# Values and compressed keys of 1024 latent rows by seven quarter products of 400 columns, context rows by a walk over the contraction

## The chip, the cores and the metric

The kernel runs on one core of one Trainium2 chip. The metric is the device time of one execution in microseconds (us). All matrix work is done in a split of 32-bit floats: every operand is kept as a rounded high part and a low part that holds the rest, and a product of two operands is three matmuls (high by high, low by high, high by low), which the helper `mm3` issues.

## The reference, cut to what matters

The layer takes 1024 latent rows and 256 context rows of 1024 numbers: a gated feed-forward half step, one normalised input for two attentions, their merge, and a second half step. The change lies in the input projection of the second part:

```python
qa, ka, va, cq, ckv, kr, gates = jnp.split(h @ w_in, IN_SPLITS, axis=-1)
kv = heads(_rmsnorm(ckv, g_kv) @ w_ukv, N_HEADS_MLA)
```

`va` (512 columns, the values of neighbourhood attention, 8 heads of 64), `ckv` (256 columns, the compressed keys of latent attention) and `kr` (32 columns, its rope keys) are needed for all 1280 rows, so 800 columns of `h @ w_in` over a contraction of 1024. `ckv` is then normalised row by row and multiplied by `w_ukv` for heads of keys and values.

## The kernel before, in words

Engines run their own instruction streams. The kernel is written as one plan: `plan.step` appends a step of TensorE work, and `plan.spread(fs, x, y)` puts side work (casts, subtractions, loads) between the steps numbered x and y. All DMAs are issued by one queue, that of SyncE, in the order of the program; an issue whose data isn't there yet holds up all behind it. `store` hands a write to the queue two steps late. Wide tiles of 128x1024 come from two pools ("u" with 24 buffers and "v" with 16), tiles of 128x512 from a third ("t" with 20), and PSUM banks from three tags (s3, m3 and v2).

A weight piece is loaded, ScalarE casts it to its high part, and VectorE subtracts that for the low part (`split`, `high_low`). The rows of `h` stand the other way round in planes of 128x512 (8 blocks of the contraction by two halves of the rows). `h2` is the planes of the latent rows for the quarter products that stand ahead of this place: a11, a12 and a22, and the sums s1 to s4 of the seven-product scheme. The plane a21 (blocks 0 to 3, rows 512 to 1023) is not among the seven. Before, `fill1` (L467) made its high and low part for the work here and wrote them out through `keep21` (`k21`, 8 stores), and `load21` brought them back.

The work that changes is two sets of ten steps, one step per 128 rows (eight latent tiles, then two context tiles, whose columns come from `hc2`, filled from `xcs` by `hc2_step`):

- `lat_tile(s, t)`: 8 blocks of the contraction by 3 matmuls of 288 columns (ckv and kr). The result is copied out, the row's scale is found (`rstd`), and `scale_row` multiplies and stores the tile to `cks`; `latent_steps` loads the ten tiles back.
- `va_tile(s, t)`: 8 blocks by 3 matmuls of 512 columns, then a cast and a subtraction of 128x512 and 8 stores of 32x8x128 to the four key windows `vws` (one for each block of 16 query columns; rows of 512 bytes, 128 KB a store, 8 tiles by 8 stores). A context tile is one store to `vcs`.

Between the stores of the values the queue issues the four `winT` loads of 512 KB. `side_weight` splits them, and `side_k` takes them for the NA keys of the context rows, four steps right behind the last `va_tile`. Then follow `kv_heads` for the chunks 2 (context), 0 and 1 and `q_heads`. `latent_cols` turns the scaled keys by TensorE. `q_stat` is a step of 8 thin matmuls for the norm of the query rows, put behind the second step of the stage. The seven-product scheme itself (`Quarters`) serves other products of the kernel with quarters 512 columns wide: in its first two products it copies four banks to SBUF with ScalarE (`out`), and in the other five it adds the banks onto them with VectorE.

## Time and profile before

| What | Value |
|---|---|
| median of 3 runs | 2558.57 us (2557.13 to 2559.03) |
| the profiled execution's own time | 2559.15 us |
| its span | 2557.4 us, so 1.75 us lie outside it |
| granted TensorE clock | 0.998 |
| TensorE busy | 2529.0 us (99% of the span), 13416 matmuls |
| VectorE busy | 1936.8 us (76%) |
| ScalarE busy | 1262.8 us (49%) |
| first matmul of the first `lat_tile` | 1157.64 us after the span's start |
| first matmul of the first `side_k` | 1249.42 us |

The table is read from the totals and from the order of TensorE's matmuls in time. A busy TensorE means matmuls one behind the other; "x24" in a row of the timeline counts the matmuls that the row holds, and names such as `bm`, `bs` and `bv` are PSUM banks, `xu`, `xv` and `t` tiles of the pools, `d` memory of the chip.

### The profile page before, as it was taken

Reading aid. Unit: us, or ns where it says so; the run is one execution under the profiler, and the core shown is the slowest. Engines: PE = TensorE matmul, PEld = TensorE weight load, DVE = VectorE, ACT = ScalarE, POOL = GpSimd, SP = SyncE. Lnnn points to the kernel's source line nnn. Section 1 sums busy time; section 2 is a strip of 40 time slices with the busy share of each in tenths; the row PEclk is TensorE's granted clock in tenths of the full one; section 3 lists DMA queues with packets and bytes.
Section 4 is the critical chain, followed back from the end, with each engine's and each line's share of the span. In section 5 each row is a group of like instructions: output and inputs, shape, how many; then the busy total and the mean of one; then the engine's idle time right before and its main releaser. Section 6 shows DMA issues by size and latency. Waiting matters only on the chain.

```text
span 2557.4 us, 38229 instructions
## 1 busy us (share of the span) xinstructions
PE 2529.0 (99%) x13416; PEld 2159.6 (84%) x13416; DVE 1936.8 (76%) x3629; ACT 1262.8 (49%) x2375; POOL 218.6 (9%) x372
## 2 busy tenths in 40 slices
PE   8999999999999999999999999999999999999998
PEld 6888888888898888889889999998888888888887
DVE  4789996887786577874568988887886888767777
ACT  5632233445654753433448988783266322233444
POOL 1000000001000000001003522221011000000003
PEclk9999999999999999999999999999999999999999
DMA  8455643943674666755978733206836445326724
GB/s 307 153 177 190 200 146 119 340 146 132 226 272 141 212 232 222 242 183 177 302 282 292 232 91 77 68 7 244 311 131 211 156 157 169 111 99 234 273 70 165
DMA packets 245761, 479.47 MB, mean 187 GB/s; under 512 B 30465, under 2 KB 71617, under 8 KB 245569
## 3 DMA queue, kind: packets, MB, share of 16 engines
q1 hardware_dynamic: 245568, 477.02, 55.5%
q8 instruction: 106, 1.74, 0.3%
q14 instruction: 87, 0.70, 0.1%
HBM read 348.93 MB, written 127.99 MB: 186 GB/s over the span
## 4 chain that ended last, share of the span: by engine, by line
PE 84%; ACT 6%; DVE 6%; issue 3%; DMA 1%; POOL 0%; SPq 0%; POOLq 0%; DVEq 0%; ACTq 0%
PE bs L154 36%; PE bm L154 26%; PE bv L154 19%; PE bm L157 2%; ACT xu L1914 2%; DVE xu L1778 2%; DVE t L1941 1%; ACT t L1940 1%; ACT t L120 1%; PE bs L157 1%; DVE xv L120 1%; DVE xu L120 1%; ACT t L1914 1%; DVE t L120 1%; ACT xu L120 0%
## 5 line engine op out<-in xcount | busy, mean ns | idle before, releaser
L120 ACT CAST xu<-t 128x512 fp32r<-128x512 f32 (+1 forms) x270 | 161.4, 603 | 493.4 <-DVE t L120 351.3
L154 PE MATMUL bm<-xu,xu 128*128 128x512 f32 (+2 forms) x1572 | 366.6, 386 | 0.0
L154 PE MATMUL bs<-xv,xu 128*128 128x512 f32 x1488 | 357.4, 389 | 0.3 <-DVE t L120 0.3
L154 PEld LDWEIGHTS bm<-xu,xu 128*128 128x128 f32 x1572 | 288.0, 188 | 56.7 <-ACT t L120 0.2
L154 PE MATMUL bv<-xv,xu 128*128 128x512 f32 x1342 | 335.5, 389 | 0.0
L154 PEld LDWEIGHTS bs<-xv,xu 128*128 128x128 f32 x1488 | 279.1, 188 | 59.0 <-issue 1.1
L154 PEld LDWEIGHTS bv<-xv,xu 128*128 128x128 f32 x1342 | 251.8, 188 | 52.2
L154 PE MATMUL bs<-xv,xv 128*128 128x512 f32 x1086 | 265.9, 390 | 0.0
L120 DVE TENSOR_TENSOR xu<-xu,xu 128x512 fp32r<-128x512 f32 (+1 forms) x296 | 202.3, 688 | 59.2 <-ACT xu L120 58.7
L154 PEld LDWEIGHTS bs<-xv,xv 128*128 128x128 f32 x1086 | 203.0, 188 | 41.7
L154 PE MATMUL bs<-xu,xu 128*128 128x512 f32 (+1 forms) x972 | 226.2, 381 | 0.0
L120 DVE TENSOR_TENSOR t<-t,t 128x512 f32<-128x512 f32 (+2 forms) x278 | 185.3, 674 | 45.1 <-ACT t L120 36.1
L154 PE MATMUL bs<-w,w 96*128 96x512 f32 (+3 forms) x832 | 206.9, 368 | 3.1 <-DMA w<-d 1.8
L154 PEld LDWEIGHTS bs<-xu,xu 128*128 128x128 f32 x972 | 177.4, 188 | 35.7 <-issue 1.4
L120 POOL TENSOR_SCALAR st<-st 128x1 f32<-128x1 f32 (+1 forms) x66 | 34.7, 526 | 1888.7 <-ACT t L120 1870.4
L120 ACT CAST xv<-t 128x512 fp32r<-128x512 f32 x170 | 106.1, 624 | 167.5 <-PE bv L154 69.0
L120 DVE TENSOR_TENSOR xu<-t,xu 128x512 fp32r<-128x512 f32 (+1 forms) x270 | 179.5, 665 | 10.7 <-ACT xu L120 10.6
L154 PE MATMUL bm<-xv,xv 128*128 128x512 f32 x690 | 182.9, 390 | 0.0
L120 ACT CAST xu<-xu 128x512 fp32r<-128x512 f32 x218 | 133.2, 619 | 74.0 <-DMA xu<-in_wo 46.6
L120 DVE TENSOR_TENSOR xv<-t,xv 128x512 fp32r<-128x512 f32 x170 | 117.2, 690 | 65.0 <-ACT xv L120 64.5
L154 PE MATMUL bv<-t,w 128*128 128x256 f32 x896 | 150.2, 288 | 2.2 <-DVE t L1941 1.6
L154 PEld LDWEIGHTS bm<-xv,xv 128*128 128x128 f32 x690 | 129.2, 188 | 27.1 <-issue 0.4
(246 smaller groups left out, 4238.2 us busy)
## 6 DMA issues: line engine op xcount, KB each, us to landing
d<-t SPq DMA_DIRECT2D x366, 256.0 KB, 2.6
t<-d SPq DMA_DIRECT2D x274, 256.0 KB, 3.9
xu<-in_f1w SPq DMA_DIRECT2D x59, 512.0 KB, 4.2
xu<-in_f2w SPq DMA_DIRECT2D x58, 512.0 KB, 3.8
t<-in_wada SPq DMA_DIRECT2D x112, 256.0 KB, 5.2
xv<-in_f1w SPq DMA_DIRECT2D x44, 512.0 KB, 6.8
xu<-in_winT SPq DMA_DIRECT2D x38, 512.0 KB, 4.9
w<-d SPq DMA_DIRECT2D x32, 512.0 KB, 6.3
```

Source lines behind the costliest of these rows:

```text
L120: return lambda *x, **y: pin(f(*x, **y))
L154: return pin(nc.tensor.matmul(o, s, m, start=start, stop=stop, skip_group_check=open_group[0]))
L157: return pin(nc.tensor.transpose(o, x, i))
L1778: nc.vector.tensor_scalar(dst, src, 1.0, FMIN, op0=ALU.mult, op1=ALU.max, accum_out=m)
L1914: nc.scalar.activation(x, x, AF.Exp, bias=n_[:, s:s + 1], accum_out=l[:, i:i + 1])
L1940: nc.scalar.copy(t[0], pb)
L1941: nc.vector.tensor_tensor(t[1], pb, f32(t[0]), op=ALU.subtract)
```

## The change

`TokenQuarters` takes the 1024 latent rows by the seven-product scheme. The 800 columns are put in two halves of 400: the first is values 0 to 383 and 16 columns of `ckv`, the second the other 240 columns of `ckv`, the 32 of `kr` and values 384 to 511. With the two halves of the contraction and the two halves of the rows that makes four quarters on each side. Each of the seven products has four blocks of the contraction by four row tiles by three matmuls of 400 columns, a step per block, so 28 steps. Left operands are planes of `h2` that exist already. Right operands are the weight quarters b11, b21, b12 and b22 and four sums t1 to t4 (16 subtractions by VectorE). A weight block is loaded by two DMAs, of which eight have rows of 16 columns. The a21 plane is neither kept nor loaded.

A row tile is complete when its last product is: tiles 0 to 3 behind the fifth, 4 to 7 behind the seventh. The fifth, sixth and seventh products gather in the same four banks: the fifth ends with step 19, the sixth with step 23, behind each VectorE adds the banks onto SBUF, and the seventh goes on a row tile at a time (steps 24 to 27), each in one bank. `done(t)` then copies the rope keys, finds the scale, and makes the values' high and low parts in two pieces (6 heads and 2 heads), with the stores of before. The compressed keys stay in SBUF, `cks` is gone.

The context rows are eight steps (`context_step`), one for each block of the contraction: two row tiles by three matmuls of 512 and three of 288 columns, into four banks that stay open for eight steps. Their weights are loaded a second time, in four pairs (`context_load`). `hc2_step` moves to steps 17 to 24 of the token part, the order of the heads becomes 0, 1, 2, and the `winT` loads are put at steps 3 to 6 of the context part, into pool "v".

On SyncE's queue the last loads ahead of `side_k` stand like this before (`d_369` to `d_372` are the four windows, and a name `xu_...` the values of one row tile, two stores to each window):

```order
L132 DMA d_369<-xu_11510 32x8x128 x2
L132 DMA d_370<-xu_11510 32x8x128 x2
L132 DMA d_371<-xu_11510 32x8x128 x2
L132 DMA d_372<-xu_11510 32x8x128 x2
L132 DMA xu_11662<-in_winT 128x1024
L132 DMA d_369<-xu_11567 32x8x128 x2
L132 DMA d_370<-xu_11567 32x8x128 x2
L132 DMA d_371<-xu_11567 32x8x128 x2
L132 DMA d_372<-xu_11567 32x8x128 x2
L132 DMA xu_11709<-in_winT 128x1024
```

and now like this:

```order
L132 DMA d_368<-xu_11610 32x8x128 x2
L132 DMA d_369<-xu_11610 32x8x128 x2
L132 DMA d_370<-xu_11610 32x8x128 x2
L132 DMA d_371<-xu_11610 32x8x128 x2
L132 DMA d_368<-xu_11657 32x8x128 x2
L132 DMA d_369<-xu_11657 32x8x128 x2
L132 DMA d_370<-xu_11657 32x8x128 x2
L132 DMA d_371<-xu_11657 32x8x128 x2
L132 DMA xv_11775<-in_winT 128x1024
L132 DMA xv_11812<-in_winT 128x1024
L132 DMA xv_11833<-in_winT 128x1024
L132 DMA xv_11847<-in_winT 128x1024
```

The four loads stood behind the values of tiles 3, 4, 5 and 6; now all four stand behind the values of the last latent tile. The first stores themselves stand on the same queue between the loads of the context weights, now:

```order
L132 DMA xv_11402<-in_wva 128x1024
L132 DMA xv_11404<-in_wc 128x704
L132 DMA d_368<-xu_11340 32x8x128 x2
L132 DMA d_369<-xu_11340 32x8x128 x2
L132 DMA d_370<-xu_11340 32x8x128 x2
L132 DMA d_371<-xu_11340 32x8x128 x2
L132 DMA d_368<-xu_11375 32x8x128 x2
L132 DMA d_369<-xu_11375 32x8x128 x2
L132 DMA d_370<-xu_11375 32x8x128 x2
L132 DMA d_371<-xu_11375 32x8x128 x2
L132 DMA xv_11497<-in_wva 128x1024
L132 DMA xv_11499<-in_wc 128x704
```

The pair behind the stores of tiles 0 and 1 is blocks 2 and 3 of the context weights; the pair of blocks 4 and 5 comes behind tiles 2 and 3, that of blocks 6 and 7 behind tile 4. Before, these weights were one load for all ten tiles and stood ahead of every store.

On VectorE the values' low parts stood with the splits of later weights before (128x8x64 is a row tile's values, `xu_11470` a high and low part for the heads):

```order
L120 TENSOR_TENSOR xu_11438<-bs_11413,xu_11438 128x8x64
L120 TENSOR_TENSOR xu_11467<-bm_11442,xu_11467 128x8x64
L120 TENSOR_TENSOR xu_11470<-xu_11408,xu_11470 128x512
L120 TENSOR_TENSOR xu_11473<-xu_11408,xu_11473 128x512
L120 TENSOR_TENSOR xu_11510<-bs_11485,xu_11510 128x8x64
```

and now, where the sixth product ends and the seventh begins (`bs_11211` to `bm_11214` are its four banks, `xv_11427` and `xv_11429` the low parts of the last two weight blocks):

```order
L120 TENSOR_TENSOR xu_11375<-xu_11054,xu_11375 128x2x64
L120 TENSOR_TENSOR xv_11380<-xu_10848,xv_11380 128x400
L120 TENSOR_TENSOR t_11252<-t_11398,t_11248 128x256
L120 COPY kr<-xu_11056 128x32
L120 TENSOR_SCALAR xu_11054<-xu_11054,st_11372 128x256
L120 TENSOR_TENSOR xu_11414<-xu_11056,xu_11414 128x6x64
L120 TENSOR_TENSOR xu_11414<-xu_11056,xu_11414 128x2x64
L120 TENSOR_TENSOR xu_10971<-xu_10971,bs_11211 128x400
L120 TENSOR_TENSOR xu_10973<-xu_10973,bs_11212 128x400
L120 TENSOR_TENSOR xu_10975<-xu_10975,bs_11213 128x400
L120 TENSOR_TENSOR xu_10977<-xu_10977,bm_11214 128x400
L120 TENSOR_TENSOR xv_11427<-xu_10873,xv_11427 128x400
```

The adds that free the banks, and the low parts for the last steps, stand behind the values of tile 2, whose casts come from ScalarE.

The diff, cut to its core:

```diff
         ORDER = (("a11", "b11"), ("a12", "b21"), ("s1", "t1"), ("s4", "b22"), ("s2", "t2"), ("s3", "t3"), ("a22", "t4"))
         BANKS = (("s", "s", "s", "m"), ("m", "m", "v", "v"))
-        LAST = 4
+        WIDTH, SECOND, YKEY = 512, 512, "v"
...
-    def lat_tile(s, t):
-        pb = s.product(t)
-        x = T2()
-        vec.tensor_copy(x[:, :288], pb)
-        vec.tensor_copy(kr[:, t, :], x[:, 256:288])
-        scale_row()
-        scaled_rows.append((t, x[:, 0:256], rstd(x[:, 0:256], 256)))
-
-    def va_tile(s, t):
-        pb = s.product(t)
+    def latent_out(t, x, keys):
+        vec.tensor_copy(kr[:, t, :], keys)
+        scale_latent()
+        ck[t] = x
+        scaled.append((x, rstd(x, 256)))
+    def values_out(t, pieces):
         v = U(F32R)
         vv = v.rearrange("p (h c) -> p h c", h=NH)
-        pv = pb.rearrange("p (h c) -> p h c", h=NH)
-        split_to(vv[:, :, 0:64], vv[:, :, 64:128], pv)
+        for h, src in pieces:
+            pv = src.rearrange("p (h c) -> p h c", c=64)
+            hs = slice(h, h + pv.shape[1])
+            split_to(vv[:, hs, 0:64], vv[:, hs, 64:128], pv)
...
+    class TokenQuarters(Quarters):
+        WIDTH, SECOND, YKEY = 400, 400, "u"
...
+        def load_b(self, name, p):
+            t = self.slot(name, p)
+            k = 4 * (int(name[1]) - 1) + p
+            v, c = (k % 2) * 512, (k % 2) * 352
+            if name[2] == "1":
+                ld(t[:, 0:384], a["wva"][k // 2][:, v:v + 384])
+                ld(t[:, 384:400], a["wc"][2][k // 2][:, c + 64:c + 80])
+            else:
+                ld(t[:, 0:272], a["wc"][2][k // 2][:, c + 80:c + 352])
+                ld(t[:, 272:400], a["wva"][k // 2][:, v + 384:v + 512])
+        def cast(self, n):
+            self.raw[n] = cast(self.slot(self.ORDER[n // 4][1], n % 4), self.WIDTH, "t" if n < 16 else "v")
+        def split(self, n):
+            x, src = self.raw.pop(n)
+            low(*x, src)
+            self.sp[n] = self.h.f[self.ORDER[n // 4][0]][n % 4], x
+        def plan(self, plan):
+            o = len(plan.main)
+            for n in range(self.n):
+                x = min(o + n - 3, o + self.tail[n][0] - 1 if n in self.tail else o + n)
+                plan.early(lambda n=n: self.cast(n), x)
+                plan.spread([lambda n=n: self.split(n)], x, x + 1)
+                plan.step(lambda n=n: self.step(n))
+            for p in range(4):
+                for name, x in (("b11", p - 7), ("b21", p - 3), ("b12", p - 3), ("b22", p + 2)):
+                    plan.spread([lambda name=name, p=p: self.load_b(name, p)], o + x, o + x + 1)
+                for name, x in (("t1", 2), ("t2", 9), ("t3", 13), ("t4", 16)):
+                    plan.spread([lambda name=name, p=p: self.sum(name, p)], o + x + p, o + x + p + 1)
+            return o
+        def done(self, t):
+            y = self.ys[t]
+            latent_out(t, y[:, 384:640], y[:, 640:672])
+            values_out(t, ((0, y[:, 0:384]), (6, y[:, 672:800])))
+    cxr, cxw, cxb = {}, {}, {}
+    def context_load(j):
+        cxr[j] = load(a["wva"][j], key="v"), load(a["wc"][2][j], 704, "v")
+    def context_split(k):
+        v, c = cxr[k // 2]
+        o = (k % 2) * 512, (k % 2) * 352 + 64
+        cxw[k] = split(v[:, o[0]:o[0] + 512], 512, "v"), split(c[:, o[1]:o[1] + 288], 288, "v")
+    def context_step(k):
+        if k == 0:
+            for t in range(2):
+                cxb[t] = PB("v"), PB("m")[:, :288]
+        open_group[0] = True
+        for t in range(2):
+            for pb, w in zip(cxb[t], cxw[k]):
+                mm3(pb, hc2[0].get(k, t * P, P), w, k == 0, k == KD - 1)
+        open_group[0] = False
+        del cxw[k]
+        if k == KD - 1:
+            for t in range(2):
+                x = T2()
+                vec.tensor_copy(x[:, :288], cxb[t][1])
+                latent_out(8 + t, x[:, 0:256], x[:, 256:288])
+            for t in range(2):
+                values_out(8 + t, ((0, cxb[t][0]),))
...
-    sets = [(2, Set(a["wc"][2], 352, "u", "v", 64), range(10)), (None, Set(a["wva"], 512, "v", "u"), range(10))]
+    plan.spread([lambda: ld(rope, a["rope"])], len(plan.main) - 2, len(plan.main) - 1)
+    ys3 = {}
+    tokens = TokenQuarters(h2, ys3)
+    lat_at = tokens.plan(plan)
     o = len(plan.main)
-    lat_at = o
-    plan.spread(sets[0][1].loads(), o - 9, o - 3)
-    plan.spread(sets[0][1].steps(), o - 5, o)
-    plan.spread([load_c, load21, lambda: ld(rope, a["rope"])], o - 2, o)
-    ck = {}
-    for x, (c, s, ts) in enumerate(sets):
-        o = len(plan.main)
-        for t in ts:
-            plan.step((lambda s=s, t=t: va_tile(s, t)) if c is None else (lambda s=s, t=t: lat_tile(s, t)))
-        if x == 0:
-            plan.spread([lambda k=k: hc2_step(k) for k in range(KD)], o + 2, o + 7)
-        if x + 1 < len(sets):
-            plan.spread(sets[x + 1][1].loads(), o, o + 1)
-            plan.spread(sets[x + 1][1].steps(), o + 1, len(plan.main))
-    va_at = o
+    c_at = o
+    plan.step(*[lambda k=k: context_step(k) for k in range(KD)])
+    plan.spread([load_c], lat_at + 13, lat_at + 14)
+    def context_banks(x):
+        banks[0] = x
+    plan.spread([lambda: context_banks("mm")], lat_at + 16, lat_at + 17)
+    plan.spread([lambda k=k: hc2_step(k) for k in range(KD)], lat_at + 17, lat_at + 25)
+    plan.spread([lambda: context_banks("ss")], c_at, c_at + 1)
+    plan.spread([lambda: context_banks("ms")], c_at + 8, c_at + 9)
+    for j in range(4):
+        plan.spread([lambda j=j: context_load(j)], c_at - 6 + 2 * j, c_at - 5 + 2 * j)
+        plan.spread([lambda j=j: tokens.done(j)], lat_at + 20 + j, lat_at + 21 + j)
+        plan.spread([lambda j=j: tokens.done(4 + j)], lat_at + 25 + j, lat_at + 26 + j)
+    for k in range(KD):
+        plan.spread([lambda k=k: context_split(k)], c_at - 3 + k, c_at - 2 + k)
...
-    lat = {(ci, "c"): latent_steps(ci, ck, cks, 256) for ci in range(3)}
...
-    o = va_at
-    plan.spread([scale_row], o, o + 1)
-    plan.spread([f for ci in (2, 0, 1) for f in [lat[ci, "c"]]], o + 3, o + 4)
-    plan.spread([lambda k=k: raw_load(("kv", k), a["wukv"][k]) for k in range(2)], o, o + 1)
-    plan.spread([lambda k=k: wukv.append(kv_weight(k)) for k in range(2)], o + 2, o + 4)
-    plan.spread([f for ci in (2, 0, 1) for f in calls(latent_cols(ci, 6, 8, ck, "u", ckv[ci]), 2)], o + 6, o + 10)
-    plan.spread([lambda i=i: raw_load(("k", i), a["winT"][4 + i]) for i in range(4)], o + 6, o + 10)
-    plan.spread([lambda i=i: side_weight(i) for i in range(4)], o + 8, o + 12)
+    o = c_at
+    plan.spread([lambda k=k: raw_load(("kv", k), a["wukv"][k]) for k in range(2)], o - 4, o - 3)
+    plan.spread([lambda k=k: wukv.append(kv_weight(k)) for k in range(2)], o, o + 2)
+    plan.spread([scale_latent], o + 1, o + 2)
+    for ci, x in ((0, 2), (1, 4), (2, 9)):
+        plan.spread(calls(latent_cols(ci, 6, 8, ck, "u", ckv[ci]), 2), o + x, o + x + 2)
+    plan.spread([scale_latent], o + 8, o + 9)
+    plan.spread([lambda i=i: raw_load(("k", i), a["winT"][4 + i], 1024, "v") for i in range(4)], o + 3, o + 7)
+    plan.spread([lambda i=i: side_weight(i) for i in range(4)], o + 6, o + 10)
     plan.step(*[lambda i=i: side_k(side_w[i], i) for i in range(4)])
     o = len(plan.main)
-    plan.step(*calls(kv_heads(2, ckv[2]), 7))
-    plan.spread([lambda d=d: xq.append(load(cqx[d], key="v")) for d in range(6)], o - 4, o - 2)
-    plan.spread([lambda d=d: q_cols(0, d) for d in range(6)], o - 2, o + 7)
+    plan.step(*calls(kv_heads(0, ckv[0]), 9))
+    plan.spread([lambda d=d: xq.append(load(cqx[d], key="v")) for d in range(6)], o - 3, o)
+    plan.spread([lambda d=d: q_cols(0, d) for d in range(6)], o, o + 9)
     o = len(plan.main)
-    plan.step(*calls(kv_heads(0, ckv[0]), 9))
+    plan.step(*calls(kv_heads(1, ckv[1]), 9))
     plan.spread([lambda k=k: raw_load(("q", k), a["wuq"][k], QR) for k in range(6)], o - 6, o + 6)
     plan.spread([lambda k=k: wuq.append(q_weight(k)) for k in range(6)], o - 3, o + 9)
     o = len(plan.main)
-    plan.step(*calls(kv_heads(1, ckv[1]), 9))
-    plan.spread([lambda d=d: q_cols(1, d) for d in range(6)], o + 2, o + 14)
+    plan.step(*calls(kv_heads(2, ckv[2]), 7))
+    plan.spread([lambda d=d: q_cols(1, d) for d in range(6)], o, o + 12)
     plan.spread([lambda: qrow.append(gate_rows(qstat[1]))], len(plan.main) - 2, len(plan.main) - 1)
     plan.step(*calls(q_heads(0, cqn[0]), 9))
```

91 lines of the change are left out of this document (19 added, 72 removed).

## The prediction

> **What bounds the kernel now.** I read the page's totals first, then the chain of work that ended last.
>
> ```profile
> span 2557.4 us, 38229 instructions
> PE 2529.0 (99%) x13416; PEld 2159.6 (84%) x13416; DVE 1936.8 (76%) x3629; ACT 1262.8 (49%) x2375; POOL 218.6 (9%) x372
> PE 84%; ACT 6%; DVE 6%; issue 3%; DMA 1%; POOL 0%; SPq 0%; POOLq 0%; DVEq 0%; ACTq 0%
> ```
>
> TensorE is the bound: 28 us of the span aren't its work. The change touches one stage, from the first `lat_tile` to the first `side_k`. So I read TensorE's timeline there.
>
> ```profile
> 1157.64 3.32 PE L154 MATMUL bm<-xu,xu 128*128 128x288 f32 x24
> 1160.80 3.32 PE L154 MATMUL bs<-xu,xu 128*128 128x288 f32 x24
> 1167.12 0.38 PE L157 MATMUL bs<-ident,xv 128*128 128x128 f32 x2
> 1167.34 0.38 PE L157 MATMUL bm<-ident,xv 128*128 128x128 f32 x2
> 1167.55 1.84 PE L154 MATMUL bv<-strip,t 128*128 128x1 f32 x16
> 1169.26 3.01 PE L154 MATMUL bs<-xu,xu 128*128 128x288 f32 x21
> 1192.77 5.62 PE L154 MATMUL bm<-xv,xu 128*128 128x512 f32 x24
> 1198.22 1.98 PE L154 MATMUL bs<-xv,xu 128*128 128x512 f32 x8
> 1249.42 11.75 PE L154 MATMUL bm<-t,xu 128*128 128x256 f32 x96
> ```
>
> A tile starts 3.16 us behind the one before it, so a matmul of 288 columns takes 131.7 ns; 5.45 us make 227 ns for 512 columns. The turns for `hc2` take 0.22 us a block, `q_stat` 1.7 us. I count from T0 = 1157.64: `side_k` starts at T0+91.8. Next, what the other engines and the DMAs do in this stage (columns: window, its length and TensorE, its weight loads, VectorE, ScalarE, GpSimd, granted clock, DMA share, GB/s):
>
> ```profile
> 1157.60:1192.80 35.20, 35.20 (x274) 35.16 (x274) 18.47 (x47) 16.94 (x44) 8.79 (x21) 1.00 0.43 153
> 1192.80:1249.40 56.60, 56.60 (x261) 46.92 (x261) 15.04 (x30) 11.56 (x23) 0.74 (x2) 1.00 0.84 226
> 1261.00:1290.00 29.00, 29.00 (x149) 24.41 (x148) 24.34 (x44) 22.18 (x46) 0.00 (x0) 1.00 0.98 352
> ```
>
> TensorE is full from end to end and VectorE and ScalarE are half free, but the DMAs are 84% busy in the second half, and 98% in the heads that follow. So the stage has a second bound close below. What fills it are the 64 stores of the values:
>
> ```profile
> 1210.80 12.40 SPq L132 DMA_DIRECT2D d<-xu  x24
> 1211.00:1223.00 12.00, 12.00 (x55) 9.93 (x54) 4.70 (x12) 2.22 (x4) 0.00 (x0) 1.00 0.97 254
> DMA packets 5987, 3.04 MB, mean 254 GB/s; under 512 B 371, under 2 KB 5987, under 8 KB 5987
> ...
> DMA packets 743, 2.06 MB, mean 411 GB/s; under 512 B 82, under 2 KB 82, under 8 KB 743
> 1226.00:1250.00 24.00, 24.00 (x120) 20.02 (x119) 6.84 (x12) 6.24 (x13) 0.00 (x0) 1.00 1.01 290
> ```
>
> The first three are a stretch with these stores alone (three tiles, 24 stores): 0.517 us a store, with the DMA engines 97% busy at 254 GB/s, so the engines are the limit and not the issue. The fourth is a stretch of 4 us from 1159 on with loads in rows of 4 KB: 411 GB/s. The fifth mixes both, and adding up fits it: 6.96 MB, of which four `winT` loads are 2.10 MB and take 5.1 us at 411, the other 4.86 MB take 19.1 us at 254, in sum 24.2 of 24.0 us.
>
> **The change part by part.**
>
> *TensorE's work.* Removed: 240 matmuls of 288 columns (31.6 us) and 240 of 512 (54.5 us), 86.1 us. Added: 7 x 4 x 4 x 3 = 336 matmuls of 400 columns. The trace has none; between 131.7 and 227 ns a straight line gives 131.7 + 112 x 0.425 = 179.3 ns, in sum 60.2 us. Context: 8 x 2 x 3 = 48 of each old kind, 17.2 us. Together 77.4 us, 8.7 us less. It lies wholly on the path, since TensorE never waits here. `q_stat` (1.7 us) and the turns of `hc2` (8 x 0.22 = 1.7) are issued in both; what is left of the 91.8, 2.3 us, are the 20 turns of the scaled keys. Sixteen of them (1.8) stand ahead of `side_k` still, and 0.5 us go behind it.
>
> *VectorE and ScalarE in the quarters.* Added are 28 low parts, 16 sums and 20 adds of 400 columns on VectorE, about 0.56 us each by the rows below and the 288-column low part's smaller size: 36 us; 16 low parts go (about 9 us). With the 33.5 us of the two windows that is some 60 of 77 us. ScalarE goes from 28.5 to about 45 us. Both fit, so I cost their work at nothing as long as its order holds; TensorE is the cover.
>
> ```profile
> 1161.49 0.42 ACT L120 ACTIVATE t<-t 128x256 bf16<-128x256 f32 x1 [1.96 <-DVE t L120]
> 1161.82 0.19 ACT L120 ACTIVATION_READ_ACCUMULATOR t<-t 128x1 f32 x1
> 1168.23 1.00 ACT L120 ACTIVATE t<-bs,mod,a 128x256 f32<-128x256 f32 x2
> 1198.42 0.59 ACT L120 CAST xu<-bm 128x512 fp32r<-128x512 f32 x1 [4.37 <-PE bm L154]
> 1199.05 0.69 DVE L120 TENSOR_TENSOR xu<-bm,xu 128x512 fp32r<-128x512 f32 x1 [5.14 <-ACT xu L120]
> ```
>
> *Bank hand-overs.* Where a product follows another in the same four banks, bank 0 was finished 9 matmuls earlier: 1.6 us, against one copy or add of 0.6. No wait, while VectorE comes at once. At step 24 it doesn't: the add that frees bank 0, and the low parts of the last two blocks, stand behind the values of tile 2, whose casts stand on ScalarE behind the two activations of `hc2`. The price is between 0 and what is queued, 0.69 + 4 x 0.56 + 2 x 0.56 = 4.0 us. I take 1.6, since VectorE works this queue off while the sixth product still runs.
>
> So TensorE would be ready for `side_k` at 60.2 + 17.2 + 1.7 + 1.7 + 1.8 + 1.6 = T0+84.2, 7.6 us earlier, of which 0.5 come back: -7.1.
>
> *The stores of the values.* They were spread over `va_tile`, from 1199.76 on. Now the first is possible when tile 0 is whole, behind step 19, and ScalarE gets to it only behind the activations of `hc2` whose turns stand behind step 20: 21 x 2.15 = 45.2, plus 1.7 and 4 x 0.22 make T0+47.8; then 1.0, 0.42 + 0.19, 0.6 and 0.7 of the rows above, and a wait or two on VectorE: T0+51. From there 64 stores are 33.0 us by the row of 24. Tiles come faster (one per step of 2.15 us) than their 4.1 us of transfer, so the DMA engines stay full.
>
> *The `winT` loads.* All four now stand on SyncE's queue behind the 64 stores, and so do three of the four pairs of context weights (0.52 + 0.36 = 0.885 MB each) and `wukv` (1.05 MB). Ahead of the end of the first `winT` load are 2.65 + 1.05 + 0.52 = 4.2 MB, 10.3 us at 411. So it ends at 51 + 33.0 + 10.3 = T0+94.3; with about 1.2 us until the landing is seen and the cast and low part (0.6 + 0.7, of which the low part is needed later), `side_k` starts at about T0+96. The context steps that wait for their pairs (blocks 4 and 6, some 2 us) lie inside this wait. Transfer times, for scale:
>
> ```profile
> xu<-in_winT SPq DMA_DIRECT2D x4, 512.0 KB, 4.9
> xu<-in_wukv SPq DMA_DIRECT2D x2, 512.0 KB, 3.9
> xu<-in_wc SPq DMA_DIRECT2D x4, 32.0 KB, 2.2
> ```
>
> The last row is the nearest to the eight new loads of 16 columns (8 KB). They are issued four steps and more ahead, 8 us against 2.2: nothing. If they were ten times as slow they would hold the first steps by up to 5 us.
>
> *What goes without a gain.* The 20 transfers of `cks` and the 12 of the kept plane were on no path that TensorE waited for. Those of `cks` were 2.6 MB on the DMAs of this stage; they leave room there, but ahead of T0+51, where there is room already. The heads' order changes nothing in amount. The `wuq` loads, behind the same queue, come 1 to 3 us late to heads whose DMAs were 98% busy: between 0 and 4 us, and I take 1.
>
> *The sum,* against the profiled execution's 2559.15 us (0.6 above the median of the runs): `side_k` from T0+91.8 to T0+96, +4.3; turns behind it +0.5; heads +1. 2559.15 + 5.8 = **2565 us**. The gain of 7.1 us on TensorE is there, and a wait of 11 to 12 us for `winT` is more.
>
> **The rivals.**
>
> *The stores don't limit, the kernel is faster.* If they moved at the 411 GB/s of the loads, 8.39 MB would take 20.4 us and not 33.0, the first `winT` would be in at T0+82 to 83, and TensorE wouldn't wait: 2559.15 - 7.1 = 2552. It decides at about 370 GB/s: from there on more than 5 us of gain are left. Against it is the row of 254 GB/s at a share of 97%, the same pieces in the same direction. For it speaks that nothing says how much of that share is the reads of other work.
>
> The Trainium skill's page "DMA: Bandwidth & Descriptors" (section Specifications) puts the piece from which a transfer runs at line rate at 512 bytes, which is the size of a row of these stores, and the limit of a core at about 358 GB/s. By it the 64 stores would take an estimated 23.4 us, and the kernel would be at 2554 to 2556. The trace disagrees: 254 GB/s for pieces of 512 bytes against 411 for rows of 4 KB, both with full engines.
>
> *Gain and wait cancel.* If the first store goes out 4 to 6 us earlier than I have it (ScalarE takes tile 0 ahead of the `hc2` activations), the wait shrinks to 6 or 7 us: 2558 to 2561. Against it: both stand in ScalarE's own order, activations first.
>
> *The heads pay as well.* The backlog lasts 5 us longer than before when the heads begin, and `xq` and `wuq` (6 loads each) feed splits on a VectorE busy 24.34 of 29 us. If the splits come late by the whole backlog and not by a part of it, the heads add 5 to 8 us: 2569 to 2573.
>
> **How the numbers follow.** 0.2% (5.1 us) is about what a measurement of this kernel can tell from no change: same is 2553.5 to 2563.7. My forecast (2561 to 2569) has 0.47, of which 0.09 lie within the bound; the faster rival 0.19, 0.02 of it within; cancelling 0.18; the heads 0.16. So faster 0.17, same 0.29, slower 0.54. The likeliest case alone is 2561 to 2569; the range takes in most of the others: 2552.5 to 2571.
>
> **What would show it.** Right: a wait of TensorE of some 10 us ahead of the first `side_k`, ended by `winT`'s landing through ScalarE; no idle time of TensorE in the first 24 steps; 400-column matmuls 179 ns apart; the DMAs near full from T0+51 to T0+95 at 250 to 300 GB/s. A wait of 1 to 2 us at step 24 would be the tail. Wrong: stores above 350 GB/s, `side_k` at T0+84, or idle time inside the quarters, for which I have no price.

## The result and the profile after

The changed kernel takes 2570.79 us (median of 6 runs, 2569.12 to 2571.78), the kernel before 2557.70 in runs beside it: a ratio of 1.0053, 95% interval 1.0042 to 1.0063. It is slower by 13 us. The profiled execution took 2570.67 us, its span is 2568.9, against 2557.4 before: 11.5 us. The totals of the profile page:

```profile
span 2568.9 us, 38214 instructions
PE 2524.9 (98%) x13368; PEld 2160.0 (84%) x13368; DVE 1960.9 (76%) x3687; ACT 1275.6 (50%) x2417; POOL 224.0 (9%) x372
```

TensorE has less work by its count of matmuls and idles 44 us instead of 28. Its timeline in the stage (start, duration, what ran, and in brackets the idle time ahead and what ended it):

```profile
1157.19 1.80 PE L154 MATMUL bs<-t,xu 128*128 128x400 f32 x9
...
1159.37 1.78 PE L154 MATMUL bs<-t,xu 128*128 128x400 f32 x9
1160.99 0.70 PE L154 MATMUL bm<-t,xu 128*128 128x400 f32 x3
1161.53 1.78 PE L154 MATMUL bs<-t,xu 128*128 128x400 f32 x9
...
1213.40 1.54 PE L154 MATMUL bs<-xv,xu 128*128 128x400 f32 x7 [0.79 <-DVE xu L120]
1215.33 1.18 PE L154 MATMUL bs<-xv,xu 128*128 128x400 f32 x5 [0.38 <-DVE xv L120]
...
1216.49 4.57 PE L154 MATMUL bs<-xv,xu 128*128 128x400 f32 x24
1220.89 2.32 PE L154 MATMUL bm<-xv,xu 128*128 128x400 f32 x12
1223.06 0.86 PE L154 MATMUL bv<-xv,t 128*128 128x512 f32 x3
...
1235.54 1.95 PE L154 MATMUL bv<-xv,t 128*128 128x512 f32 x3 [2.72 <-ACT xv L120]
...
1257.04 8.57 PE L154 MATMUL bm<-t,xu 128*128 128x256 f32 x48 [8.50 <-ACT xu L120]
1265.45 0.38 PE L157 MATMUL bm<-ident,t 128*128 128x128 f32 x2
...
1271.63 1.55 PE L154 MATMUL bm<-xu,xu 128*128 128x512 f32 x6
...
1300.16 1.64 PE L154 MATMUL bs<-xu,xu 128*128 128x512 f32 x6 [1.14 <-DVE t L120]
...
1303.62 2.42 PE L154 MATMUL bs<-t,xu 128*128 128x256 f32 x18
```

Before, the rows that answer to the last two (the first product of the heads, then of `q_heads`) are these:

```profile
1261.01 0.88 PE L154 MATMUL bm<-xu,xu 128*128 128x256 f32 x6
...
1290.44 2.42 PE L154 MATMUL bs<-t,xu 128*128 128x256 f32 x18
```

The token part is what was forecast: it ends 65.9 us behind its first matmul, with 1.2 us of wait at step 24 and 180 ns for a matmul of 400 columns (the 12 of a step in 2.16 us, from 1159.37 to 1161.53). Then come a wait of 2.7 us in the context steps and one of 8.5 us ahead of `side_k`. The queue of SyncE and the cast that lets `side_k` go, and the windows (columns as in the prediction):

```profile
1208.12 8.42 SPq L132 DMA_DIRECT2D d<-xu  x16
...
1218.61 11.27 SPq L132 DMA_DIRECT2D d<-xu  x16
...
1230.99 5.52 SPq L132 DMA_DIRECT2D d<-xu  x8
...
1251.88 1.80 SPq L132 DMA_DIRECT2D xv<-in_winT  x4
```

```profile
1256.37 1.14 ACT L120 CAST xu<-xv 128x512 fp32r<-128x512 f32 x2 [10.44 <-issue]
```

```profile
1222.00:1232.00 10.00, 10.00 (x58) 8.96 (x57) 7.64 (x21) 4.98 (x14) 6.97 (x4) 1.00 1.04 304
1232.00:1238.00 6.00, 3.28 (x13) 2.41 (x13) 2.42 (x5) 2.88 (x7) 0.00 (x0) 0.77 1.07 306
...
1248.50:1257.10 8.60, 0.10 (x2) 0.06 (x1) 0.08 (x1) 0.73 (x2) 0.00 (x0) 0.72 0.98 277
1252.30:1262.50 10.20, 5.46 (x24) 5.23 (x25) 4.66 (x11) 4.15 (x10) 1.64 (x4) 0.50 0.96 339
1257.10:1266.00 8.90, 8.90 (x53) 8.67 (x54) 6.96 (x15) 5.19 (x14) 1.64 (x4) 0.70 0.97 328
1262.50:1266.00 3.50, 3.50 (x31) 3.50 (x31) 2.38 (x5) 1.76 (x5) 0.00 (x0) 1.00 1.02 258
```

The first store goes out at T0+50.9, the first `winT` at T0+94.7, it is cast at T0+99.2, and `side_k` starts at T0+99.85 (T0 is the stage's first matmul, here 1157.19). The granted clock behind the wait is 0.70 (0.50 up to 1262.5, then 1.00), and 48 matmuls that take 5.8 us at full clock take 8.4.

The runs below are compared by three starts on TensorE, counted from T0 as read from each run's own timeline. They vary far less than the whole time: before, and in the two variants of it that leave the path alone, `q_heads` starts at 132.80 each time, while the rest, from `q_heads` to the end, spreads from 1264.6 to 1270.5 us without a pattern (but for the last two runs).

| | `side_k` | its four steps | heads | `q_heads` | median us (before beside it) |
|---|---|---|---|---|---|
| before | 91.78 | 11.59 | 29.43 | 132.80 | |
| after | 99.85 | 14.59 | 31.99 | 146.43 | 2570.79 (2557.70) |
| winT first | 91.56 | 13.61 | 33.74 | 138.91 | 2563.31 (2556.29) |
| loads first | 88.18 | 13.49 | 37.42 | 139.09 | 2563.48 (2556.29) |
| kept busy | 99.32 | 14.32 | 31.67 | 145.31 | 2571.23 (2556.29) |
| before, winT last | 93.36 | 17.41 | 29.44 | 140.21 | 2565.69 (2556.29) |
| half the stores | 85.03 | 12.62 | 31.46 | 129.11 | 2554.08 (2557.12) |
| before, half the stores | 91.78 | 11.59 | 29.43 | 132.80 | 2556.28 (2557.12) |
| before, weights twice | 91.77 | 11.59 | 32.96 | 136.32 | 2560.41 (2557.12) |
| loads and wuq first | 88.25 | 16.03 | 36.98 | 141.26 | 2563.18 (2557.12) |
| rows of 4 KB | 99.21 | 14.76 | 32.41 | 146.38 | 2568.98 (2557.08) |
| rows of 4 KB, winT first | 91.56 | 13.40 | 33.62 | 138.58 | 2562.16 (2557.08) |
| before, rows of 4 KB | 91.78 | 11.60 | 29.42 | 132.80 | 2557.00 (2557.08) |
| one pair of weights | 94.23 | 14.31 | 32.27 | 140.81 | 2564.33 (2557.08) |
| stores by GpSimd | 96.79 | 21.61 | 31.38 | 149.78 | 2575.19 (2556.82) |
| the same, 4 KB | 93.82 | 19.98 | 31.87 | 145.67 | 2572.24 (2556.82) |
| stores of 64 KB | 95.66 | 14.82 | 32.94 | 143.42 | 2568.06 (2556.82) |
| a quarter, one pair | 85.06 | 12.62 | 32.12 | 129.80 | 2555.16 (2556.82) |
| stored once | 85.05 | 12.63 | 32.36 | 130.04 | 2584.06 (2556.62) |
| stored once, wuq first | 85.05 | 12.63 | 31.70 | 129.38 | 2582.94 (2556.62) |

### The profile page after: what moved, and what is told of

Its sections match the earlier page's. It is cut to its first block, busy times and chain, and to the rows that moved or that the text cites. A ratio compares the mean times of both kernels' runs of the same rounds, so it can differ in the third digit from the quotient of the medians.

```text
span 2568.9 us, 38214 instructions
## 1 busy us (share of the span) xinstructions
PE 2524.9 (98%) x13368; PEld 2160.0 (84%) x13368; DVE 1960.9 (76%) x3687; ACT 1275.6 (50%) x2417; POOL 224.0 (9%) x372
## 4 chain that ended last, share of the span: by engine, by line
PE 38%; ACT 5%; DVE 5%; issue 2%; DMA 1%; SPq 0%; POOL 0%; POOLq 0%; DVEq 0%; ACTq 0%
PE bs L154 17%; PE bm L154 11%; PE bv L154 8%; ACT xu L1926 2%; DVE xu L1790 2%; PE bm L157 2%; DVE t L1953 1%; ACT t L1952 1%; DMA t<-in_wada 1%; ACT t L1926 1%; ACT t L1766 0%; DMA xu<-in_wuq 0%; ACT t L120 0%; PE bs L157 0%; DVE xu L120 0%
## 5 line engine op out<-in xcount | busy, mean ns | idle before, releaser
L154 PE MATMUL bm<-xu,xu 128*128 128x512 f32 (+1 forms) x1500 | 356.6, 391 | 0.0
L154 PE MATMUL bs<-xv,xu 128*128 128x512 f32 (+1 forms) x1452 | 347.6, 388 | 1.5 <-DVE xu L120 0.8
L154 PEld LDWEIGHTS bm<-xu,xu 128*128 128x128 f32 x1500 | 278.2, 188 | 56.8 <-ACT t L120 0.4
L154 PE MATMUL bs<-xv,xv 128*128 128x512 f32 (+1 forms) x1134 | 274.8, 388 | 0.0
L120 DVE TENSOR_TENSOR xu<-xu,xu 128x512 fp32r<-128x512 f32 (+4 forms) x316 | 209.9, 670 | 64.6 <-ACT xu L120 64.3
L120 DVE TENSOR_TENSOR t<-t,t 128x512 f32<-128x512 f32 (+2 forms) x278 | 185.4, 674 | 43.8 <-ACT t L120 34.5
L154 PE MATMUL bs<-xu,xu 128*128 128x512 f32 (+1 forms) x900 | 216.2, 389 | 1.1 <-DVE t L120 1.1
L154 PEld LDWEIGHTS bs<-xu,xu 128*128 128x128 f32 x900 | 167.6, 188 | 37.4 <-DVE t L120 1.6
L154 PE MATMUL bm<-xv,xv 128*128 128x512 f32 (+1 forms) x690 | 182.7, 388 | 0.0
L120 ACT CAST xu<-xu 128x512 fp32r<-128x512 f32 (+1 forms) x226 | 133.8, 602 | 74.6 <-DMA xu<-in_wo 56.9
L154 PE MATMUL bm<-t,xu 128*128 128x256 f32 (+1 forms) x1252 | 157.9, 287 | 8.5 <-ACT xu L120 8.5
L154 PEld LDWEIGHTS bm<-t,xu 128*128 128x128 f32 x1252 | 154.9, 194 | 9.0 <-ACT xu L120 8.7
```

The costliest lines, as they stand in the source:

```text
L120: return lambda *x, **y: pin(f(*x, **y))
L154: return pin(nc.tensor.matmul(o, s, m, start=start, stop=stop, skip_group_check=open_group[0]))
```

## The experiments

**Where the loads stand.** Theory: the wait at `side_k` is the place of the `winT` loads behind the stores, and the slow matmuls come of the wait. Rivals: the DMAs are the bound whatever the order; the order alone does it, backlog or not.

```diff
 # winT first
-    ... raw_load(("k", i), a["winT"][4 + i], 1024, "v") ..., o + 3, o + 7)
+    ... raw_load(("k", i), a["winT"][4 + i], 1024, "u") ..., o - 9, o - 8)
 # loads first: also
-    context_load(j) at c_at - 6 + 2 * j;  wukv at o - 4
+    context_load(j) at c_at - 8 + j (the last pair in "u");  winT at o - 5;  wukv at o - 8
```

> The changed kernel with one part moved: the four winT loads are issued ahead of the first store of the values (in tiles of pool u). Theory (the wait of 8.50 us ahead of the first side_k is the place of these loads behind the 64 stores, and the slow matmuls behind it, 8.57 us for 48 against 5.8 at full clock, come of the wait): the wait and the slow matmuls go, side_k starts at about 1248.5 us instead of 1257.04, 8.5 + 2.7 us less: 2559 to 2561. The wait of 2.7 us in the context steps stays. Rival (the DMA engines are the bound whatever the order, so the wait only moves into the heads): side_k starts earlier but the heads wait more, the kernel gains under 5 us: 2566 or more.

> The changed kernel with all loads that the stage needs ahead of the stores or behind the first tile's: the four pairs of context weights, wukv, and winT behind the stores of tile 0. Theory: TensorE has no wait from step 24 to side_k, and what the first run leaves (2.7 us of wait and some 3 us of slow matmuls in the context steps) goes too: side_k at about 1243, 2553 to 2556, some 3 to 5 us faster than the kernel before the change. Rival (the DMA engines are the bound): the heads, whose loads stand behind all 64 stores, give it back: 2561 or more.

With `winT` first the wait at `side_k` and the low clock there are gone, 8.3 us, as the theory has it; the kernel is still 7 us slower than before (ratio 1.0027, 1.0017 to 1.0037), and the 2559 to 2561 of the theory were missed. With all loads first `side_k` comes another 3.4 us earlier, and `q_heads` not at all: the heads take 37.4 us instead of 33.7. So the rival holds for what is left, as far as these two runs go. ScalarE's waits in the heads, before, then in these two runs:

```profile
ACT xu L120 <- DMA xu<-in_wuq: 1.5, 2, 1.3
```

```profile
ACT xu L120 <- DMA xu<-in_wuq: 6.9, 5, 1.6
```

```profile
ACT xu L120 <- DMA xu<-in_wuq: 8.0, 5, 1.8
```

The `wuq` loads stand behind the stores too. I read these rows so that the casts that wait for them hold up the casts that free the heads' banks; a run that issues `wuq` earlier tries it below.

**The clock.** 63 matmuls of 256 columns fill the wait:

```diff
         pb = PB("m")
+        for x in range(21 if i == 0 else 0):
+            y = hc2[0].get(x % 8)
+            mm3(pb[:, :NCTX], [z[:, 0:P] for z in y], y, True, True)
```

> The changed kernel with 63 matmuls of 256 columns more, ahead of the first side_k, whose results the first matmul of side_k overwrites: TensorE works for some 7.6 us of the 8.5 us of the wait. Theory (the granted clock falls while TensorE waits, and side_k pays for it): the 48 matmuls of side_k take 5.8 to 6.2 us instead of 8.57, and the kernel is 2.4 to 2.8 us faster than the changed kernel, about 2568, though it does more. Rival (side_k is slow for another reason, such as the casts and low parts of winT that come one by one): side_k keeps its 8.5 us, and the kernel stays at 2570 to 2572.

```profile
1255.86 2.90 PE L154 MATMUL bm<-t,xu 128*128 128x256 f32 x22 [0.22 <-DVE xu L120]
...
1259.48 0.50 PE L154 MATMUL bm<-t,xu 128*128 128x256 f32 x2 [0.72 <-ACT xu L120]
1260.53 2.89 PE L154 MATMUL bm<-t,xu 128*128 128x256 f32 x22 [0.55 <-DVE xu L120]
```

The matmuls of `side_k` run at full clock (22 in 2.9 us), so the wait is what lowers it. The time stays, and `q_heads` comes 1.1 us earlier (145.31 against 146.43): the second step now waits 1.3 us for its own part of `winT`, whose cast stands on ScalarE behind the values of the context rows. In the changed kernel the row of 48 slow matmuls has no such wait in it: the low clock hid it. The forecast of 2.4 us of gain missed.

**The order without the backlog,** in the kernel before, with all `winT` loads behind the last store:

```diff
-    ... raw_load(("k", i), a["winT"][4 + i]) ..., o + 6, o + 10)
-    ... side_weight(i) ..., o + 8, o + 12)
+    all waiting stores, then the four raw_load, at o + 8
+    ... side_weight(i) ..., o + 9, o + 13)
```

> The kernel before the change with its four winT loads moved behind all 64 stores of the values, the same order as in the changed kernel. Theory (the order alone doesn't do it; the stores must also start late, here they start at 1199.8 and are paced by the tiles): the loads are issued at about 1242, the first lands at about 1247, side_k waits 0 to 2 us: 2557 to 2560. Rival (the order alone makes the wait): a wait of 6 us or more and slow matmuls behind it, 2565 or more.

`side_k` starts 1.6 us later, as the theory has it, but its steps take 17.4 us: I had moved the splits one step back as well, so each cast stood behind the result of the step before and each step waited 1.2 us. Of the 7.4 us by which `q_heads` starts later, 5.8 are in these steps; they are that edit's, and the run says little on the order.

**Fewer stores.** Half of the windows, in both kernels, and the second load of the context weights added to the kernel before:

```diff
-            for j in range(4):
+            for j in range(2):
                 for r in range(2):
-            ld(f32(v[:, o:o + 512]), vws[j][self.h])
+            ld(f32(v[:, o:o + 512]), vws[j % 2][self.h])
 # before, weights twice
+    plan.spread([lambda j=j: extra_load(j) for j in range(4)], o + 2, o + 6)
```

> The changed kernel with half of the value stores left out: only two of the four key windows are written (32 stores of 128 KB instead of 64), and the neighbourhood attention reads these two twice, so its result is not the reference's; the work of the engines is the same. It takes 16.5 us of transfers out of the stretch. Theory A (the DMA engines set the time from the first store to q_heads, so both waits, at side_k and in the heads, are theirs): no wait at side_k, none on wuq in the heads, and the 7 us of TensorE show: 2549 to 2552 if the kernel before is at 2556 to 2558. Theory B (only the place of the winT loads behind the stores costs, the heads have a cause of their own in ScalarE's and VectorE's order): side_k on time, but 2 to 4 us stay in the heads: 2553 to 2556.

> The kernel before the change with the same half of the value stores left out (its attention too reads two windows twice). Both theories: TensorE waits for nothing in this stretch, so fewer stores are worth nothing here: within 1.5 us of the kernel before. If it is over 3 us faster, the stores cost the kernel before as well, in something other than a wait of TensorE, and the comparison with the run before this one has to be made against this one.

> The kernel before the change with the four pairs of context weights (3.5 MB, 8.6 us of transfers at 411 GB/s) loaded a second time beside its value stores, into tiles that nothing reads: this part of the change alone. Theory A (the DMA engines are as good as full from the first store to q_heads): the wuq loads come 6 to 9 us later, the heads wait, 4 to 7 us slower. Theory B (there is room): no wait at side_k, and within 1.5 us of the kernel before.

With half of the stores TensorE's gain is all there at `side_k` (85.03 against 91.78), and no wait is left; in the kernel before the same edit is worth nothing. But 1.0 us go in the four steps and 2.0 in the heads, so the kernel is 3 us faster than before (0.9989, 0.9980 to 0.9998), not 7: theory B. The weights loaded twice cost the kernel before 3.5 us, all in the heads (1.0015, 1.0007 to 1.0024), between the two theories: there was room for less than these loads. Whether their 3.5 MB or their eight places on the queue cost that, the run doesn't tell.

```diff
 # loads and wuq first: loads first, and
-    ... raw_load(("q", k), a["wuq"][k], QR) ..., o - 6, o + 6)
+    ... raw_load(("q", k), a["wuq"][k], QR) ..., o - 18, o - 12)
```

> The run with all loads of the stage first, and the six wuq loads moved ahead by 12 to 18 steps as well, so that they stand ahead of the stores of the heads' keys and values instead of between them. Theory A: the order within a full queue decides who waits, and nobody waits soon for the heads' stores; the waits for wuq go (3.7 us of idle TensorE and some 3 us of lower clock in the heads of that run), q_heads start 5 to 7 us earlier, 2555 to 2558 where that run had 2563.5. Theory B (the casts of wuq hold ScalarE up whatever the time of the loads): 2562 to 2564 as before.

No gain: the heads take 37.0 us where they took 37.4, and the four steps 2.5 us more. The time is theory B's, its reason isn't: ScalarE waits for `wuq` no more, and its longest waits there are for stores (10.1 us for `d<-xu`), as I read it because the tiles it casts into are still held by values on their way out. Moving one load ahead moved the wait to a buffer.

**What a store costs.** I had read the stores as limited by the DMA engines at pieces of 512 bytes. Four edits: all heads of a row together, so that a store has 32 rows of 4 KB; the same with `winT` first; the same in the kernel before; three pairs of weights not loaded.

```diff
 # rows of 4 KB
-    vws = [DR([NH, P, 512]) for _ in range(4)]
+    vws = [DR([P, 4, 1024]) for _ in range(4)]
-                    store(vws[j][:, q:q + 32, g:g + P]..., f32(v[o:o + 32, :])...)
+                    store(vws[j][q:q + 32, row // 4, :], f32(v[o:o + 32, :]))
 # one pair of weights
-        cxr[j] = load(a["wva"][j], key="v"), load(a["wc"][2][j], 704, "v")
+        cxr[j] = cxr[0] if j else (load(...), load(...))
```

> The changed kernel with the same 64 stores of the same bytes, but the windows are laid out with all heads of a row together, so that a store writes 32 rows of 4 KB instead of 256 pieces of 512 bytes; the attention's loads of the values, far behind, read pieces of 512 bytes instead of 2 KB. Theory A (the stores are slow by their pieces, and the DMA engines make the waits): the stores run at 350 to 410 GB/s, 21 to 24 us instead of 33, winT's first load lands some 9 to 12 us earlier, side_k waits 0 to 3 us, and about 2 to 3 us stay in the order of the heads: 2554 to 2558, as fast as the kernel before or faster. Rival (the stores are held by their issue on SyncE, about 0.5 us each whatever the pieces): the stores still take 30 us and more, and the kernel stays at 2567 or more.

> Both: stores of 4-KB rows, and the winT loads ahead of the first store (the first run of this study). Theory A: TensorE has no wait from step 24 to side_k or one under 1 us, side_k starts at 84 to 86 us behind the first matmul of the stage, the heads keep 2 to 3 us: 2553 to 2556, some 2 to 4 us faster than the kernel before. Rival (issue): about that first run's 2562 to 2564.

> The kernel before the change with the same layout of the windows. TensorE waits for no store there, so both theories: within 1.5 us of the kernel before; what it differs by is the price of the attention's loads in smaller pieces.

> The changed kernel with three of the four pairs of context weights not loaded: every context step takes its weights from the first pair, so the context rows' products are not the reference's; the engines' work is the same. It takes 2.65 MB, 6.5 us of transfers at 411 GB/s, from between the stores. Theory A (a sum of transfers in a full queue): the first winT load is issued 6 to 7 us earlier, the waits in the context steps go, side_k starts at 92 to 94 us behind the first matmul of the stage instead of 99.9, 2562 to 2565. Rival (the stores alone make the wait, the loads run beside them): side_k at 97 or later, 2568 or more.

Pieces of 4 KB bring next to nothing (99.21 against 99.85), against my theory and for the rival; with `winT` first as well `q_heads` starts at 138.58, as with `winT` first alone (138.91), so the 2553 to 2556 us of that theory were missed too; the kernel before keeps its time with either layout. Three pairs less bring `winT` 5.6 us forward (issued at T0+89.0), as a sum of what stands in the queue. To tell bytes from stores, the next edit keeps 64 stores and halves each:

```diff
 # stores of 64 KB, on top of rows of 4 KB
-                    store(vws[j][q:q + 32, row // 4, :], f32(v[o:o + 32, :]))
+                    store(vws[j][q:q + 32, row // 4, :], f32(v[o:o + 32, 0:512]))
```

> The changed kernel with 64 value stores of half the bytes (32 rows of 2 KB: four of the eight heads; the attention takes these for the others too, so its result is not the reference's). If the stores are held by their bytes, 24 of them behind each other take 6 to 8 us on SyncE instead of 13.1 to 13.9, and side_k comes 9 us earlier or more: 2556 to 2561. If they are held by something per store (issue, completion), they keep 0.40 to 0.46 us each, and the kernel stays at 2564 to 2569.

The queue's last 24 stores after the change, with 4-KB rows, and with half the bytes:

```profile
1237.60 13.87 SPq L132 DMA_DIRECT2D d<-xu  x24
```

```profile
1235.35 13.11 SPq L132 DMA_DIRECT2D d<-xu  x24
```

```profile
1236.03 11.84 SPq L132 DMA_DIRECT2D d<-xu  x24
```

0.58, 0.55 and 0.49 us a store, waits included. In the last case the DMA engines are far from full (the share of the queue in a stretch of these stores, with half the bytes and after the change):

```profile
q1 hardware_dynamic: 963, 1.41, 62.0%
```

```profile
q1 hardware_dynamic: 5167, 3.13, 99.8%
```

The time of an issue alone, without the waits ahead of it (shortest, median and longest in ns), of all 64 stores after the change, with 4-KB rows, and with half the bytes:

```profile
L132 SPq DMA_DIRECT2D d<-xu x64: 302/472/1632, 1208.1 to 1251.0; - x64
```

```profile
L132 SPq DMA_DIRECT2D d<-xu x64: 302/420/784, 1205.8 to 1248.0; - x64
```

```profile
L132 SPq DMA_DIRECT2D d<-xu x64: 302/424/581, 1207.8 to 1247.4; - x64
```

So a store of 32 rows takes 0.42 us of SyncE's queue at 64 KB and at 128 KB, and one in pieces of 512 bytes 0.47, or 0.52 with the pause to the next; that the engines were 97% busy with the latter stood beside it. In the changed kernel, though, the rows of the 64 stores (8.42, 11.27, 5.52 and 13.87) add up to 39.1 us, 0.61 each. Part of the difference is waits of the queue until loads that stand ahead have landed:

```profile
SPq L132 <- DMA xu<-in_wukv: 1.9, 2, 1.0
SPq L132 <- DMA xv<-in_wc: 1.3, 2, 0.7
SPq L132 <- DMA xv<-in_wva: 0.7, 1, 0.7
```

These are 3.9 us after the change and 9.1 with rows of 4 KB, so what the larger pieces save in the issues, 64 times 0.05 us, is lost again in these waits. Why an issue waits for an earlier landing was not tried. The Trainium skill's page "DMA: Bandwidth & Descriptors" (section Specifications) puts line rate at pieces of 512 bytes and more; the rows of 4 KB, which bring no time, agree with it in that pieces weren't the limit, but the time it led to (23 us for the stores) didn't come, as it speaks of bytes and not of the issue.

**Another queue.** GpSimd issues the stores:

```diff
-        return pin(nc.sync.dma_start(dst, src))
+        e = nc.gpsimd if <dst is one of vws> else nc.sync
+        return pin(e.dma_start(dst, src))
```

> The changed kernel with the 64 value stores issued by GpSimd instead of SyncE, so that no load stands behind them on its queue; bytes and pieces as they are. Theory A (the place in SyncE's queue makes the wait at side_k; the DMA engines take both queues in turn): winT's loads are issued at 75 to 80 us behind the first matmul of the stage instead of 94.7, side_k starts at 86 to 90 us, the heads keep 2 to 3 us: 2555 to 2561. Rival (the DMA engines are full, and it doesn't matter in which queue a load stands): side_k at 95 or later, 2566 or more.

> The same with stores of 4-KB rows (32 pieces a store instead of 256). Theory A: as the run before, at most 2 us faster: 2554 to 2559. If issuing 256 pieces a store holds GpSimd up, this run is clearly faster than that one.

`winT` is issued at T0+82.3, and yet the kernel is slower still (1.0071, and 1.0060 with rows of 4 KB); theory A missed in both. GpSimd makes the row scales, and they now stand behind its stores, with VectorE behind them:

```profile
1215.86 8.12 POOL L134 DMA_DIRECT2D d<-xu  x14
```

```profile
1227.92 0.35 DVE L120 TENSOR_SCALAR xu<-xu,st 128x256 f32<-128x256 f32 x1 [8.28 <-POOL st L120]
```

**The heads, and 8 stores for 64.**

```diff
 # a quarter, one pair: range(1) for j in the stores, and one pair of weights
 # stored once
-    vws = [DR([NH, P, 512]) for _ in range(4)]
+    vrows = DR([NLAT, 1024])
-            (the 8 stores of a tile)
+            store(vrows[t * P:(t + 1) * P, :], f32(v))
-            ld(f32(v[:, o:o + 512]), vws[j][self.h])
+            x = vrows.rearrange("(g q w) (h c) -> q w g h c", g=4, q=4, h=NH)
+            for q in range(4):
+                ld(f32(v[q * 32:(q + 1) * 32, o:o + 512])..., x[q, KSTART[j]:KSTART[j] + 32, :, self.h, :])
 # stored once, wuq first: wuq at o - 13 to o - 1
```

> The changed kernel with one of the four windows stored and one of the four pairs of context weights loaded (the results are not the reference's; the engines' work is the same): 25 us of stores and 6.5 us of loads less, so the queue is as good as free in this stretch. Theory A (the queue also makes the heads late): from the first head's matmul to q_heads 29.4 to 30.2 us, as before the change (29.43). Theory B (the heads' order and the turn of ScalarE's casts make them late): 31 us or more, as with half of the stores (31.46).

> The changed kernel, with each row tile's values written once as a whole (8 stores of 512 KB instead of 64 of 128 KB in four overlapping windows), and the windows cut out by the attention's loads (128 loads of 64 KB instead of 32 of 256 KB). The result is the full one. Theory (SyncE hands out a store in 0.4 to 0.5 us whatever it holds, so 64 of them hold all loads behind for 30 us): the wait at side_k goes, side_k starts at 85 to 87 us behind the first matmul of the stage, q_heads at 129 to 130, as with half or a quarter of the stores: 2553 to 2556 if the new loads cost the attention nothing, up to 3 us more if they do. Rival (the order on the queue makes the wait whatever the stores): side_k at 92 or later, 2561 or more.

> The same with the six wuq loads issued 7 steps earlier. If the 2 to 2.7 us that stay in the heads come from ScalarE's casts waiting for wuq (3.8 us of such waits with a quarter of the stores), the first head's matmul to q_heads takes 29.5 to 30.5 us instead of 31.5 to 32, and the kernel gains 1 to 2 us on the run before. If they come from the order of the heads (the context's short products last), it stays at 31.5 or more, and the time within 1 us.

With the queue as good as free the heads still take 32.1 us, so their 2 to 3 us aren't the backlog's: theory B. TensorE's waits of 0.2, 1.1 and 0.55 us stand at the context's short products, which now come last. That points at the heads' order, but no run puts the old order back, so it isn't shown. Eight whole stores in place of 64, with the full result, put `side_k` at 85.05 and `q_heads` at 130.04, 2.8 us ahead of the kernel before: the cause is confirmed in the stage. These stores write half the bytes too, as each value goes out once; but the 64 stores of 64 KB write as little, and so do the 32 of half the stores, and `side_k` starts at 95.66 with 64 stores, at 85.03 with 32 and at 85.05 with 8. So their number counts for more than their bytes, which at 64 stores of whole rows are worth 3.6 us (99.21 against 95.66). Issuing `wuq` earlier brings 0.7 us of the heads back (32.36 to 31.70), so most of their 2.9 us isn't the wait for it. But the attention behind loses 29 us with the 128 smaller loads; TensorE's largest wait in that run:

```profile
PE bs L154 <- DVE st L1812: 23.2, 22, 2.3
```

VectorE's and ScalarE's instructions there stand in another order than in the changed kernel. Whether that or the loads makes this wait was not tried, and stays open. No variant with the full result beats the kernel before.

## Why the prediction was right or wrong

The direction and the mechanism were right: TensorE's gain is there and a wait for `winT` behind the 64 stores is more. The first store was put at T0+51 and came at 50.9; the tail at step 24 was put at 1.6 and cost 1.2; TensorE would be ready at T0+84.2, and with the queue out of the way it is at 85.05. A matmul of 400 columns takes 180 ns, where 179 was put. The time, 2570.8, lies at the end of the range. The size was off by a factor of two: 6 us against 13. By the terms of the sum:

- **"`side_k` starts at about T0+96"**: 99.85. From the first store to `winT`'s issue it took 43.8 us; I had 33.0 for the stores and 9.0 for the loads ahead of it. That total came near by luck, as I had added up transfers, and the time went on 64 issues, on those of the loads, and on waits for loads to land. From the issue to the cast it took 4.5 us, where I had 2.5 (1.3 of transfer, and 1.2 until the landing is seen, which no row shows): the load stands in engines that are still full, with a share of 0.98. Sum +3.9.
- **`side_k` itself had no term** but 0.5 us of turns. It took 14.6 us instead of 11.6: the clock behind a wait of 8.5 us, which I hadn't asked for at all, though I forecast the wait. With the queue free it is 12.6, so 2.0 lie at the clock and what it hides, and the rest at the turns and a wait for the second part of `winT`. Beyond my term +2.5. The Trainium skill's page "TensorE: Matmul & The Clock Gate" (Part 1) has the clock at half after an idle window of about 3.4 us, and full again after a busy one as long. The trace has it down already after a wait of 2.72 us (0.77 in that window), and back 5.5 us after the wait of 8.5 us ended (0.50 up to 1262.5).
- **"Heads +1"**: +2.6, and the runs show no part of it to be the backlog's, by which I had priced it: in the four runs of the changed kernel with fewer stores, where `side_k` has no wait ahead of it, it is 2.0 to 2.9, and 2.7 with the queue as good as free. What is left is what I had put at nothing, "the heads' order changes nothing in amount"; the waits stand where the order changed, but that it is the order is not shown.

These make 8.0 beyond my 5.8, against 13.6 us by which `q_heads` starts later; 2 us of that are absent in the profiled span (the stage starts 0.45 earlier, and the rest is 1.7 shorter, as much as it varies between runs of the same code).

**"The engines are the limit and not the issue"** was wrong as a reason, though the 0.517 us were right as a price for stores alone: with half the bytes the 24 stores still take 0.49 us each. It misled as to a cure: larger pieces brought nothing. Two readings were wrong and touch no sum: the stretch at 411 GB/s is 5 us long and not 4, and loads that take ten times 2.2 us, issued 8 us ahead, would hold the first steps by 14 us and not by 5.

The faster rival (stores at the loads' rate) fell with the stores' pace; cancelling fell too. The rival that the heads pay as well came nearest in time, 2569 to 2573, but by another sum: the heads took 2.6 us more and not 5 to 8, and no less with the queue free.

## What to carry to other kernels

Where loads and stores share one queue, count its entries as well as its bytes: here a store cost nearly half a microsecond of the queue at 64 and at 128 KB, and a load behind 64 of them and eight other loads went out 44 us after the first. A change that makes results complete late, all together, takes the cover from the transfers that carried them off one at a time, and what waits is not the stores but the loads behind. When you forecast a wait of TensorE of several microseconds, price the clock behind it as well, and look what the slow matmuls hide.

## What the runs showed that I had not expected

A wait of 2.72 us was enough to bring the granted clock down (0.77 in that window). With `winT` first even one of 1.92 us in the heads was followed by six matmuls of 512 columns in 2.56 us, where 1.36 is full speed. Stores with rows of 4 KB were hardly faster than with pieces of 512 bytes (0.55 against 0.58 us), though their issue alone was (0.42 against 0.47): the queue waited for loads to land instead. A wait that was filled with matmuls brought the clock back and only 1.1 us, as the next thing in line was 1.3 us late. And on GpSimd's queue, 14 stores held a scale of one row up by 8 us, and with it VectorE and TensorE.
